# The high parts of the filling channel's weights: cast on GpSimd in place of ScalarE

## Chip, cores and metric

One core of a Trainium2 chip (trn2). The metric is the device time of one execution in microseconds (us). A program of this kernel has five instruction queues that matter here: TensorE (PE, with PEld for its weight loads), VectorE (DVE), ScalarE (ACT), GpSimd (POOL) and SyncE (SP), which issues most of the loads. Each runs its own instructions strictly in the order written into its queue, and waits where an operand is not ready.

## What is computed

A two-layer encoder over 512 tokens of width 1024. Per layer the normed input `h` is projected to five mixers (three kinds of softmax attention, a linear recurrence with a state per head, and attention over a memory of 256 tokens), each mixer's output is projected by its own rows of `w_branch` and weighted by a gate, and the sum goes through `w_out`, a residual and a layer norm:

```python
for i, (o, wdt) in enumerate(zip(branch_outs, BRANCH_WIDTHS)):
    proj = jnp.einsum('bsc,cd->bsd', o, w_branch[start:start + wdt])
    gate = jax.nn.sigmoid(jnp.einsum('bsd,de->bse', h, w_gate[:, i * d:(i + 1) * d]) + b_gate[i * d:(i + 1) * d])
    terms.append(gate * proj)
```

All of it is in float32.

## The kernel before

Every large product is done as three products of rounded operands. A weight tile arrives as float32 (`wraw`), is split into a high part (`whi`, a cast to the rounded type float32r) and a low part (`wlo`, the raw value minus the high part), and `gemm3_steps` (L145) issues for each block of 128 input rows the three matmuls high*high (L149), high*low (L150) and low*high (L151), 512 columns each.

Weights come through two channels, named by a letter: `r` for the projections that stand first in a stage, and `f` for the ones that fill: the gates and the branch projections of `branch_steps` (L370), the second projection of a pair in the first attention mixer, its `silu2`, and the memory's keys and values (`memory_kv`, L260). `load_w` (L120) loads 128x512 pieces from the SP queue into `wrawr` or `wrawf` (two buffers each); `split_w` (L129) makes the high part on ACT (L135) and the low part on DVE (L136), in `whir`/`wlor` or `whif`/`wlof`, two buffers each. A piece of 512 columns feeds four blocks, that is twelve matmuls. A buffer of `whif` is free again once its last L150 matmul is done, one of `wrawf` once its low part is made.

A layer has three parts. First the attention mixers (before 520 us, and 1110 to 1620 us in the profile). Then the recurrence (520 to 1075, and 1620 to 2170 us): `early` (L802) prepares a head pair, `late` (L945) runs a chain of small DVE operations that inverts triangular blocks (L963 multiplies into `pr`, L965 adds into `W`) and a chain of small matmuls, with many small ACT copies between. As the recurrence alone would leave PE idle, `fill` (L396) runs the gates and branch projections of four of the five mixers beside it, one block of three matmuls at a time (`pull`, L404). The gate's product stands in one PSUM buffer `pf`; ACT reads it by a Tanh (`gt`, L380), and only then the branch's product takes the same buffer. Last the fifth mixer's gates, `w_out` and the layer norm.

POOL has little: a cast of a mask table (L321), six memsets per two layers, and DMA issues (`k_stack`, L435 and L437, which copies halves of the keys across partitions, and `reload`, L366, which fetches spilled mixer outputs `o`).

The order in each queue is set by a scheduler when the program is built; it takes instructions in the order in which it believes they become ready.

Of the kernel before, what the change touches and what calls it, by code (L numbers as in the profile page):

```python
# [52 lines left out]
def encoder_kernel(ctx: ExitStack, tc: tile.TileContext, x, mem, ln_in, rel_bias, w_in, par, w_up, a_up,  # L53
                   d_lambda, w_mem, w_branch, w_gate, w_out, lnp, cst, cossin, onehot, cnt, msk, out):
    nc = tc.nc
# [30 lines left out]
    def f(t):  # L86
        return t.bitcast(F32)
# [32 lines left out]
    def load_w(src, n, ch):  # L120
        r = []
        for o in range(0, n, 512):
            w = min(512, n - o)
            raw = wp.tile([128, 512], F32, name="wraw" + ch, tag="wraw" + ch, bufs=2)[:, :w]
            nc.sync.dma_start(out=raw, in_=src[:, o:o + w])
            r.append((raw, w))
        return r

    def split_w(src, n, ch="r", raws=None):  # L129

        r = []
        for raw, w in raws or load_w(src, n, ch):
            hi = wp.tile([128, 512], F32R, name="whi" + ch, tag="whi" + ch, bufs=2)[:, :w]
            lo = wp.tile([128, 512], F32R, name="wlo" + ch, tag="wlo" + ch, bufs=2)[:, :w]
            nc.scalar.copy(hi, raw)  # L135
            tt(lo, raw, f(hi), ALU.subtract)  # L136
            r.append((hi, lo))
        return r
# [22 lines left out]
    def proj(ps, l, blk, hT, ch="r"):  # L161
        w = split_w(w_in[l, blk], 1024, ch)
        gemm3(ps, [(*wk(w, k), hT[:, 0, k, :], hT[:, 1, k, :]) for k in range(8)])

    def proj_halves(pss, l, blks, hT, chs, ws):

        ws = ws or [split_w(w_in[l, b], 1024, ch) for b, ch in zip(blks, chs)]
        for sl in (slice(0, 256), slice(256, 512)):
            for ps, w in zip(pss, ws):
                gemm3(ps[:, sl], [(*wk(w, k), hT[:, 0, k, sl], hT[:, 1, k, sl]) for k in range(8)])  # L170
# [89 lines left out]
    def memory_kv(l, b):  # L260
        ps = ps_m()
        w = split_w(w_mem[l, b], 1024, "f")
        gemm3(ps[:, :256], [(*wk(w, k), mT[k // 2][:, 0, k % 2, :], mT[k // 2][:, 1, k % 2, :]) for k in range(8)])
        kv = wp.tile([128, S], F32, name="kv", tag="gt", bufs=1)[:, :256]
        nc.scalar.copy(kv, ps[:, :256])
        nc.sync.dma_start(out=scr_kv[l, b], in_=kv)
# [1013 lines left out]
```

## Time and profile before

| | |
|---|---|
| median of 3 runs | 2260.67 us (2260.49 to 2261.9) |
| the profiled execution | 2261.37 us |
| its span, first to last instruction | 2259.6 us |
| PE / DVE / ACT / POOL busy | 97% / 77% / 56% / 3% |
| the chain that ended last | PE 70%, DVE 14%, ACT 8%, DMA 5%, issue 3% |
| the filling channel's casts on ACT | 272, 164.4 us |
| mean granted clock of PE | 0.999 of full speed (2.4 GHz) |

Around the span the profiled execution has 1.8 us. The matmuls are pipelined: two of 512 columns that follow each other start some 0.23 us apart though each shows 0.39 us, so a busy PE may still have gaps. "The chain" is followed back from the last instruction through whatever released each step; time of an engine that is not on it costs nothing by itself.

### The profile page before, as it was taken

How to read it: one execution, taken by the hardware profiler on the slowest of the kernel's cores; microseconds unless marked ns; L12 is line 12 of the kernel's file. 1: busy time of each engine (PE TensorE's matmuls, PEld its weight loads, DVE VectorE, ACT ScalarE, POOL GpSimd, SP SyncE). 2: the span in 40 equal slices, each digit the busy share in tenths (PEclk: the TensorE clock that was granted, in tenths of full speed). 3: DMA queues.
4: the chain of work that ended last, by engine and by line, in shares of the span. 5: the costliest groups of instructions: out<-in, count | busy, mean ns of one | idle time of the engine just before them, and what ended most of it. 6: DMA issues, size and time to landing. Idle time of an engine off the chain costs nothing.

```text
span 2259.6 us, 36239 instructions
## 1 busy us (share of the span) xinstructions
PE 2186.5 (97%) x13056; PEld 1678.6 (74%) x13056; DVE 1730.6 (77%) x4236; ACT 1273.2 (56%) x2785; POOL 59.6 (3%) x117
## 2 busy tenths in 40 slices
PE   6999999999999999999999999999999999999998
PEld 5777777777767777777787777777777777777776
DVE  7677887677989797975568778766788979879565
ACT  3565666676665555644326656677675646565440
POOL 0000000100000000000000000001000000000000
PEclk9999999999999999999999999999999999999999
DMA  7732124322222221315333312333313213222261
GB/s 261 222 108 91 56 80 112 113 86 85 75 80 66 86 88 59 102 49 181 117 115 108 98 62 70 97 106 89 112 57 99 71 62 98 72 80 73 84 195 38
DMA packets 111780, 220.49 MB, mean 98 GB/s; under 512 B 13240, under 2 KB 23224, under 8 KB 111216
## 3 DMA queue, kind: packets, MB, share of 16 engines
q1 hardware_dynamic: 101456, 195.09, 27.0%
q0 software_dynamic: 10144, 23.08, 4.0%
q8 instruction: 103, 1.69, 0.3%
q14 instruction: 77, 0.63, 0.1%
HBM read 187.66 MB, written 27.31 MB: 95 GB/s over the span
## 4 chain that ended last, share of the span: by engine, by line
PE 70%; DVE 14%; ACT 8%; DMA 5%; issue 3%; DVEq 0%; POOL 0%; ACTq 0%; SPq 0%
PE pg L150 10%; PE pg L151 10%; PE pg L149 10%; PE pf L149 6%; PE pf L150 5%; PE pf L151 5%; PE psc L444 4%; PE po L489 3%; PE pt L470 3%; DVE W L965 2%; DVE pr L963 2%; DMA wrawr<-in_w_out_dram 1%; DVE wlof L136 1%; PE po L479 1%; DMA wrawf<-in_w_mem_dram 1%
## 5 line engine op out<-in xcount | busy, mean ns | idle before, releaser
L149 PE MATMUL pg<-hT,whir 128*128 128x512 f32 (+1 forms) x912 | 364.0, 399 | 3.2 <-DVE kl L436 1.4
L150 PE MATMUL pg<-hT,whir 128*128 128x512 f32 (+1 forms) x912 | 365.4, 401 | 0.5 <-DVE hT L176 0.5
L151 PE MATMUL pg<-hT,wlor 128*128 128x512 f32 (+1 forms) x912 | 363.8, 399 | 2.1 <-DVE wlor L136 2.1
L136 DVE TENSOR_TENSOR wlor<-wrawr,whir 128x512 fp32r<-128x512 f32 x240 | 163.9, 688 | 114.8 <-ACT whir L135 104.9
L135 ACT CAST whir<-wrawr 128x512 fp32r<-128x512 f32 x240 | 147.7, 618 | 175.1 <-PE pg L150 116.7
L135 ACT CAST whif<-wrawf 128x512 fp32r<-128x512 f32 (+1 forms) x272 | 164.4, 605 | 135.4 <-PE pf L150 77.9
L149 PE MATMUL pf<-hT,whif 128*128 128x512 f32 x512 | 220.8, 431 | 3.4 <-DVE gt L388 2.8
L136 DVE TENSOR_TENSOR wlof<-wrawf,whif 128x512 fp32r<-128x512 f32 (+1 forms) x272 | 181.4, 669 | 49.2 <-ACT whif L135 43.2
L150 PE MATMUL pf<-hT,whif 128*128 128x512 f32 x512 | 206.7, 404 | 0.0
L151 PE MATMUL pf<-hT,wlof 128*128 128x512 f32 x512 | 205.2, 401 | 0.0
L149 PEld LDWEIGHTS pg<-hT,whir 128*128 128x128 f32 x912 | 172.0, 189 | 40.6 <-issue 3.0
L151 PEld LDWEIGHTS pg<-hT,wlor 128*128 128x128 f32 x912 | 171.9, 188 | 40.0 <-DVE wlor L136 4.9
L150 PEld LDWEIGHTS pg<-hT,whir 128*128 128x128 f32 x912 | 171.9, 189 | 37.8 <-issue 3.9
L176 DVE TENSOR_TENSOR pT<-pt,pT 128x512 fp32r<-128x512 f32 x176 | 114.2, 686 | 34.2 <-ACT pT L175 33.1
L175 ACT CAST pT<-pt 128x512 fp32r<-128x512 f32 x176 | 94.7, 589 | 63.0 <-PE pt L470 61.7
L149 PEld LDWEIGHTS pf<-hT,whif 128*128 128x128 f32 x512 | 96.5, 188 | 35.8 <-DVE gt L388 10.2
L470 PE MATMUL pt<-cst,p 128*128 128x128 f32 x704 | 118.6, 273 | 0.5 <-DVE p L461 0.5
L151 PEld LDWEIGHTS pf<-hT,wlof 128*128 128x128 f32 x512 | 96.4, 188 | 22.2 <-issue 1.6
L963 DVE TENSOR_TENSOR pr<-W,U 128x60 f32<-128x60 f32 (+24 forms) x496 | 103.5, 209 | 11.4
L965 DVE TENSOR_TENSOR W<-W,pr 128x60 f32<-128x60 f32 (+24 forms) x496 | 102.9, 208 | 11.0
L470 PEld LDWEIGHTS pt<-cst,p 128*128 128x128 f32 x704 | 89.8, 141 | 28.4 <-DVE p L461 3.6
L150 PEld LDWEIGHTS pf<-hT,whif 128*128 128x128 f32 x512 | 96.8, 189 | 18.8 <-issue 4.3
(326 smaller groups left out, 4809.1 us busy)
## 6 DMA issues: line engine op xcount, KB each, us to landing
wrawr<-in_w_in_dram SPq DMA_DIRECT2D x224, 256.0 KB, 2.8
wrawf<-in_w_gate_dram SPq DMA_DIRECT2D x160, 256.0 KB, 2.8
o<-scr_o POOLq DMA_DIRECT2D x26, 512.0 KB, 4.5
wrawf<-in_w_branch_dram SPq DMA_DIRECT2D x48, 256.0 KB, 2.7
bias<-scr_toe SPq DMA_DIRECT2D x24, 448.0 KB, 3.3
scr_o<-os SPq DMA_DIRECT2D x20, 512.0 KB, 3.7
wrawf<-in_w_in_dram SPq DMA_DIRECT2D x32, 256.0 KB, 3.0
wrawr<-in_w_out_dram SPq DMA_DIRECT2D x32, 256.0 KB, 2.9
```

Source lines behind the costliest of these rows:

```text
L135: nc.scalar.copy(hi, raw)
L136: tt(lo, raw, f(hi), ALU.subtract)
L149: mm(ps, ah, bh, start=(i == 0), stop=False)
L150: mm(ps, ah, bl, start=False, stop=False)
L151: mm(ps, al, bh, start=False, stop=(i == n - 1))
L175: nc.scalar.copy(hi, src)
L176: tt(lo, src, f(hi), ALU.subtract)
L444: mm(ps[:, :nk], q[:, i, sl], part[:, i if g is None else g, :nk], start=(j == 0), stop=(j == 1))
L470: nc.tensor.transpose(pt[:, qb * 128:(qb + 1) * 128], p4[qb][:, kb * 128:(kb + 1) * 128], ident)
L489: mm(po, vwin(kb), pT[:, b, :], start=(kb == 0 and b == 0), stop=(kb == nkb - 1 and b == 1))
L963: tt(pr, W[:, t8, s:s + 1].to_broadcast([128, nt, n]), U[:, s:s + 1, rsl].to_broadcast([128, nt, n]), ALU.mult)
L965: tt(W[:, t8, rsl], W[:, t8, rsl], pr, ALU.add)
```

## The change

```diff
-            nc.scalar.copy(hi, raw)
+            if ch == "f":
+                nc.gpsimd.tensor_copy(hi, raw)
+            else:
+                nc.scalar.copy(hi, raw)
             tt(lo, raw, f(hi), ALU.subtract)
```

The 272 casts of channel `f` go from ACT's queue to POOL's; the 240 of channel `r` stay on ACT. Lines after L134 stand three higher in the changed kernel. The scheduler orders all queues anew.

ACT's queue in the middle of the recurrence of the first layer, where the Tanh of a gate stands at 829.46 us. Before:

```order
L1088 CAST yhi<-ys 128x512
L893 COPY NS<-pm 32x2x32
L890 COPY NS<-pm 32x128
L893 COPY NS<-pm 32x2x32
L890 COPY NS<-pm 32x128
L135 CAST whif<-wrawf 128x512
L380 ACTIVATE gt<-pf,hb 128x512
L893 COPY NS<-psc 32x2x32
```

and now:

```order
L1091 CAST yhi<-ys 128x512
L896 COPY NS<-pm 32x2x32
L893 COPY NS<-pm 32x128
L896 COPY NS<-pm 32x2x32
L893 COPY NS<-pm 32x128
L383 ACTIVATE gt<-pf,hb 128x512
L896 COPY NS<-psc 32x2x32
```

The cast that stood between the copies and the Tanh is gone, and nothing else has moved there.

POOL's queue from the start of the first recurrence to the second layer's first key copy. Before:

```order
L728 MEMSET WD 128x1024
L732 MEMSET ST_5175 128x128
L732 MEMSET ST_5176 128x128
L366 DMA o<-scr_o 128x1024 x13
L435 DMA kh<-kh 64x512
```

and now (the first rows of it):

```order
L731 MEMSET WD 128x1024
L735 MEMSET ST_5175 128x128
L735 MEMSET ST_5176 128x128
L136 CAST whif<-wrawf 128x512 x15
L369 DMA o<-scr_o 128x1024 x4
L136 CAST whif<-wrawf 128x512 x24
L369 DMA o<-scr_o 128x1024 x4
L136 CAST whif<-wrawf 128x512 x24
L369 DMA o<-scr_o 128x1024 x2
```

The casts stand between the reloads. Ten fill casts stand ahead of the memsets and fifteen behind, and the first mixer has 24, so the first gate piece of each following mixer is cast ahead of that mixer's reloads and the second piece behind them.

DVE's queue inside the inversion chain, at about 796 us. Before:

```order
L136 TENSOR_TENSOR wlof<-wrawf,whif 128x512
L965 TENSOR_TENSOR W<-W,pr 128x3x23
L963 TENSOR_TENSOR pr<-W,U 128x66
L965 TENSOR_TENSOR W<-W,pr 128x3x22
L963 TENSOR_TENSOR pr<-W,U 128x63
L965 TENSOR_TENSOR W<-W,pr 128x3x21
L963 TENSOR_TENSOR pr<-W,U 128x60
L965 TENSOR_TENSOR W<-W,pr 128x3x20
L136 TENSOR_TENSOR wlof<-wrawf,whif 128x512
```

and now:

```order
L139 TENSOR_TENSOR wlof<-wrawf,whif 128x512
L1048 COPY ST_5176<-pt 64x64
L1058 TENSOR_TENSOR SY<-pt,SY 64x256 x2
L966 TENSOR_TENSOR pr<-W,U 128x66
L968 TENSOR_TENSOR W<-W,pr 128x3x22
L966 TENSOR_TENSOR pr<-W,U 128x63
L968 TENSOR_TENSOR W<-W,pr 128x3x21
L966 TENSOR_TENSOR pr<-W,U 128x60
L968 TENSOR_TENSOR W<-W,pr 128x3x20
L966 TENSOR_TENSOR pr<-W,U 128x76
L968 TENSOR_TENSOR W<-W,pr 128x4x19
L139 TENSOR_TENSOR wlof<-wrawf,whif 128x512
```

The low parts stand a few places to either side of where they were, still among the steps of the chain.

## Rows read from the trace of the kernel before

**Rows 1.** The page: busy time of each engine, the chain by engine.

```profile
PE 2186.5 (97%) x13056; PEld 1678.6 (74%) x13056; DVE 1730.6 (77%) x4236; ACT 1273.2 (56%) x2785; POOL 59.6 (3%) x117
...
PE 70%; DVE 14%; ACT 8%; DMA 5%; issue 3%; DVEq 0%; POOL 0%; ACTq 0%; SPq 0%
```

**Rows 2.** Stretches: length, busy PE, PEld, DVE, ACT, POOL; clock, DMA share, GB/s.

```profile
170.00:520.00 350.00, 346.85 (x1628) 267.98 (x1627) 268.13 (x619) 229.83 (x474) 14.27 (x28) 1.00 0.30 89
520.00:1075.00 555.00, 539.18 (x3877) 404.69 (x3876) 446.58 (x1182) 314.44 (x734) 8.29 (x16) 1.00 0.28 88
...
1620.00:2170.00 550.00, 534.13 (x3856) 400.75 (x3855) 444.25 (x1177) 312.40 (x731) 8.35 (x16) 1.00 0.28 87
```

**Rows 3.** The page's groups: count, busy us, mean ns, idle time before and its releaser.

```profile
L135 ACT CAST whif<-wrawf 128x512 fp32r<-128x512 f32 (+1 forms) x272 | 164.4, 605 | 135.4 <-PE pf L150 77.9
...
L136 DVE TENSOR_TENSOR wlof<-wrawf,whif 128x512 fp32r<-128x512 f32 (+1 forms) x272 | 181.4, 669 | 49.2 <-ACT whif L135 43.2
```

**Rows 4.** The two recurrences, ACT's instructions on tile whif alone.

```profile
520.00:1075.00 555.00, 56.77 (x95) 1.00 0.28 88
1620.00:2170.00 550.00, 56.00 (x94) 1.00 0.28 87
```

**Rows 5.** The chain by line, in 520 to 1075 us and in 1620 to 2170 us.

```profile
by line: PE pf L149 11.0%; PE pf L150 9.0%; PE pf L151 9.0%; issue 4.1%; PE pg L150 4.0%; DVE W L965 3.9%; PE pg L151 3.9%; DVE pr L963 3.8%; PE pg L149 3.8%; DMA wrawr<-in_w_out_dram 2.7%; DVE wlof L136 2.3%; PE psc L881 2.0%; DMA wrawr<-i
...
by line: PE pf L149 11.3%; PE pf L150 9.4%; PE pf L151 9.3%; issue 4.0%; PE pg L150 4.0%; DVE W L965 3.9%; PE pg L151 3.9%; DVE pr L963 3.8%; PE pg L149 3.8%; DVE wlof L136 2.3%; DMA wrawr<-in_w_out_dram 2.2%; PE psc L881 2.0%; PE pm L881 1
```

**Rows 6.** Waits: us in total, times, longest us.

```profile
PE pf L149 <- ACT gt L380: 5.0, 12, 0.7
...
DVE wlof L136 <- ACT whif L135: 43.2, 39, 3.4
...
ACT whif L135 <- PE pf L150: 77.9, 72, 4.5
```

**Rows 7.** Timeline of DVE, POOL, PE about POOL's only cast: start, length, instruction.

```profile
21.57 1.28 DVE L236 SCALAR_TENSOR_TENSOR xt<-xt,lnmv,lngb 128x1024 f32<-128x1024 f32 x1
...
21.99 1.85 POOL L321 CAST msk<-mk 128x1152 bf16<-128x1152 f32 x1 [21.55 <-DMA mk<-in_msk_dram]
...
22.77 1.11 DVE L187 TENSOR_SCALAR rsy<-lnmv 128x2 int32<-128x2 int32 x1
...
24.52 0.39 PE L151 MATMUL pg<-hT,wlor 128*128 128x256 f32 x1 [1.19 <-DVE wlor L136]
```

**Rows 8.** POOL's memsets by shape; then L187's durations (ns min/median/max).

```profile
L728 POOL MEMSET WD<- 128x1024 f32 x2 | 2.0, 991 | 112.3 <-DMA wrawr<-in_w_in_dram 56.3 <-DVE cf L719 56.0
...
L732 POOL MEMSET ST<- 128x128 f32 x4 | 0.8, 214 | 0.0
...
L187 DVE TENSOR_SCALAR rsy<-lnmv x8: 145/156/1106, 8.6 to 2253.2; 128x2 int32<-128x2 int32 x4, 128x1 int32<-128x1 int32 x4
```

**Rows 9.** DVE in 520 to 1075 us: tiles W, wlof and wlor alone.

```profile
520.00:1075.00 555.00, 117.11 (x528) 1.00 0.28 88
...
520.00:1075.00 555.00, 62.58 (x95) 1.00 0.28 88
...
520.00:1075.00 555.00, 25.19 (x37) 1.00 0.28 88
```

**Rows 10.** The chain in order of time: start, length, what.

```profile
785.80 0.23 PE pf L151
...
828.81 0.62 ACT whif L135
...
829.46 0.70 ACT gt L380
```

**Rows 11.** Timeline at a reload: second gate cast, last issue, the gate's first matmul.

```profile
788.74 0.62 ACT L135 CAST whif<-wrawf 128x512 fp32r<-128x512 f32 x1 [0.28 <-DVE W L965]
...
789.24 0.54 POOL L366 DMA_DIRECT2D o<-scr_o  x1 [0.97 <-PE pt L1042]
...
789.94 0.50 PE L149 MATMUL pf<-hT,whif 128*128 128x512 f32 x1
```

## The prediction

> **What bounds the kernel now.** I read the page first [rows 1]: PE is busy for 97% of the span and carries 70% of the chain, DVE 14%, ACT 8%. ACT is the engine that is relieved, so the question is where ACT holds anything up, and what POOL, idle for 97%, does to others when it works. By stretches [rows 2] the attention part (170 to 520 us) is PE's: 346.85 of 350 us, so that neither a lighter ACT nor a slower DVE moves much there. The recurrences are different. PE is busy there too, but DVE is at 446.58 of 555 us, and the chain by line [rows 5] goes through DVE's small steps: W 3.9%, pr 3.8%, and the low part of the filling channel 2.3%. These two stretches also hold 95 and 94 of the 272 casts [rows 4]. So the recurrences decide, and in them DVE is the engine to watch, more than ACT. The granted clock is 1.00 in all three stretches, which is the level of 2.4 GHz, and plays no part.
>
> **What the change removes.** 272 casts of 605 ns, 164.4 us of ACT's time, and ACT's idle time ahead of them, 135.4 us, of which 77.9 us in 72 waits for PE to give a buffer of whif back [rows 3, 6]. Nothing behind such a cast on ACT could run in that time. What this is worth is what of it lies on the chain. In rows 5 the casts are not among the lines shown, the smallest of which is 2.0%; so they are at most 2.0% of 555 us and of 550 us, 22 us in both. Not all of that is given back: where the next step of the chain is the low part on DVE, the cast is needed all the same, on whichever engine. It is given back where the next step is another ACT instruction, as at 828.81 us [rows 10]: the cast, then the gate's Tanh, for which PE waits; there the Tanh would have come 0.62 us earlier. PE's waits for that Tanh are small in total, 5.0 us in 12 [rows 6]. I take a gain of 10 us, a little under half the bound, and keep 0 and 22 as its ends.
>
> **What it adds on POOL.** One row shows a POOL instruction that reads SBUF, the cast of the mask table, 1152 columns in 1.85 us [rows 7]. Scaled by columns to 512 that is 0.82 us. But it began at 21.99 us while DVE's L236, which reads two SBUF operands, ran until 22.85; from there to the cast's end at 23.84 there are 0.99 us. POOL's memsets take 991 ns for 1024 columns and 214 for 128 [rows 8], 0.87 ns a column, by which 1152 columns are 1.10 us. So I read the cast as 0.86 us of waiting for DVE and 0.99 us of work: 0.86 ns a column, 0.44 us for 512, and with some 0.1 us that the memsets show beyond their columns (214 less 128 x 0.87) 0.54 us. The ends are 0.54 and 0.82; I take 0.55, as the memsets' rate fits it. Alone, then, a cast on POOL is no dearer than the 0.605 us on ACT.
>
> **What it adds on DVE.** The same rows show the price. L187, a DVE instruction on 128x2 numbers, began at 22.77, took 1.11 us, where its median is 0.156 [rows 7, 8], and ended at 23.88, 0.04 us behind POOL's cast. The next DVE instruction, a low part, came late, and PE waited 1.19 us for it [rows 7]. So a reading POOL instruction and a DVE instruction held each other up, first DVE the cast, then the cast DVE, each for its whole length. The Trainium skill says so too (SBUF — State Buffer, "Who interferes with whom"): a DVE instruction with two SBUF inputs contends with a GpSimd instruction that reads SBUF, and whichever comes first keeps the other out to its end. The trace agrees for the case above, and shows the case of a two-input instruction that is itself kept out nowhere. If only L187's kind were kept out, by the trace alone, the sum would be that of the first rival below.
>
> In 520 to 1075 us the DVE time on tiles W, wlof and wlor alone is 117.11, 62.58 and 25.19 us [rows 9], all instructions with two SBUF inputs: 205 us, 37% of the stretch, a lower bound, as other products of SBUF tiles are not in it. Of this the chain holds 3.9 + 3.8 + 2.3 = 10.0% of the stretch [rows 5], again a lower bound; I put the other end at twice that. The terms:
>
> - On the chain. 189 casts x 15% (between 10 and 20) x 0.55 us = 16 us; ends 189 x 10% x 0.54 = 10 and 189 x 20% x 0.82 = 31.
> - Off the chain. A further 37 - 15 = 22% of 189 casts, 42 x 0.55 = 23 us of DVE delay, which meets 108 us of DVE idle time per recurrence. I take a third, 8 us; ends 0 and 23.
> - The other 83 casts stand where PE is the chain or a load is; 3 us, ends 0 and 5.
> - High parts that come later. DVE waits 39 times for whif [rows 6]. Each now has to wait out a DVE instruction (half of 0.67 us in about half the cases, 0.17 us), less the 0.05 us by which the cast is shorter: 39 x 0.12 = 5 us, of which I count half, 2; ends -3 (POOL is free sooner than ACT was) and 10.
>
> **What stands behind the casts on POOL.** The reloads and the key copies. A reload needs the last product of the mixer before it, so a cast written behind it would wait too. The order shows the first gate piece ahead of the reloads and the second behind. At 789.24 us the last issue takes 0.54 us [rows 11]; the second piece's cast would start at 789.8 in place of 788.74, and the twelve matmuls of the first piece (12 x 0.23 = 2.8 us from 789.94 [rows 10, 11]) cover it. I count 0, and 1 us a boundary, 6 in all, if that cover is gone. A load on SP waits for the low part as before. The new order of the queues as a whole (fill shifted a few steps within the recurrence) I cannot cost: 0, with 5 us to either side.
>
> **Sum.** 16 + 8 + 3 + 2 - 10 = +19 us on the profiled execution's 2261.4 us, 2280; its run lies 0.7 us above the median of 2260.67, so 2279 (+0.8%).
>
> **Rivals.**
> - Faster: two-input DVE instructions are not held up. Then the 1.85 us of the mask's cast are its own, a cast takes 0.82 us, DVE's 39 waits grow by 0.2 us each (8 us, half of it felt: 4), and ACT's gain counts up to its bound: 4 - 15 = -11, some 2250 us. For it: L236 ran its usual 1.28 us beside the cast; ACT's queue does block, 77.9 us. Against: the memsets' rate, and L187.
> - No difference: the held-up steps fall into DVE's idle time, the on-chain share is at its low end of 10 us, and ACT gives 10 back: 2261 us.
> - Much slower: a cast holds 0.82 us, at each of them DVE, at 80% busy, loses the whole of it, and the recurrence, a chain of DVE steps, can't make it up: 31 + 23 + 5 + 10 + 6 - 10 = +65, 2325 us. It decides from the point where DVE's idle time of 108 us per recurrence no longer lies where the casts fall.
>
> **Chances and range.** The forecast (2266 to 2300 us) 0.48, much slower 0.17, no difference 0.15, faster 0.20. Leaving out about a tenth on each side: 2250 to 2318 us; the likeliest case alone is 2266 to 2300. A measurement can tell some 0.2% (4.5 us) from no change: faster 0.20, same 0.15, slower 0.65.
>
> **What would show it.** Right: POOL busy up by 150 us or more, its casts between 0.55 and 1.2 us long with the longer ones beside two-input DVE work; DVE's mean for W and pr above 0.21 us, or gaps ahead of them that POOL ends; DVE's share of the chain up from 14%, ACT's down from 8% by about half a point; PE's busy time unchanged but its gaps in the recurrences longer. Wrong: W and pr at their old means beside the casts (then the first rival), the two recurrences as long as before, or the time lost in the attention part, which would mean POOL's queue and not DVE.

## The result: 2.4% slower, and the profile after

The changed kernel takes 2313.95 us (median of 4 runs, 2311.86 to 2314.4) against 2260.94 us (4 runs) of the kernel before on the same chip: ratio 1.0236, 95% interval 1.0224 to 1.0249, or +53 us. The sign was right, and the outer range (2250 to 2318 us) holds the time, near its upper end. The likeliest case (2266 to 2300 us) does not hold it, and the size was wrong: +53 us where the sum gave +19.

The page after, busy time by engine and the chain by engine; these answer to [rows 1]:

```profile
PE 2204.3 (95%) x13056; PEld 1691.6 (73%) x13056; DVE 1776.5 (77%) x4236; ACT 1131.0 (49%) x2513; POOL 265.9 (12%) x389
...
PE 68%; DVE 17%; issue 6%; ACT 5%; DMA 3%; POOL 1%; SPq 0%; DVEq 0%; ACTq 0%; POOLq 0%
```

POOL took over 206 us, ACT gave up 142. On the chain ACT fell from 8 to 5% and DVE rose from 14 to 17%. PE is 95% busy in place of 97, so it waits more. The groups that answer to [rows 3] (columns: busy us, mean ns, idle time before and its releaser), with the two steps of the inversion chain:

```profile
L136 POOL CAST whif<-wrawf 128x512 fp32r<-128x512 f32 (+1 forms) x272 | 206.7, 760 | 1477.3 <-PE pf L153 949.5
...
L139 DVE TENSOR_TENSOR wlof<-wrawf,whif 128x512 fp32r<-128x512 f32 (+1 forms) x272 | 182.4, 671 | 61.2 <-POOL whif L136 51.0
...
L968 DVE TENSOR_TENSOR W<-W,pr 128x60 f32<-128x60 f32 (+24 forms) x496 | 114.4, 231 | 12.4
L966 DVE TENSOR_TENSOR pr<-W,U 128x60 f32<-128x60 f32 (+24 forms) x496 | 109.9, 222 | 12.5
```

The list of waits after (us in total, times, longest us), which answers to [rows 6]:

```profile
DVE wlof L139 <- POOL whif L136: 51.0, 53, 3.2
...
PE pf L152 <- DVE gt L391: 17.3, 18, 1.5
...
PE pf L152 <- ACT gt L383: 4.8, 13, 0.7
...
PE pg L152 <- DMA o<-scr_o: 3.9, 3, 1.9
```

DVE waits for the high part a little longer than before (51.0 us against 43.2), and PE for DVE's product gt (17.3 us; 2.8 in the trace before). PE hardly waits for ACT's Tanh, before or after. The last line is new: PE waits 3.9 us for reloaded mixer outputs, whose issues stand behind casts in POOL's queue.

How POOL and DVE hold each other up is seen in the timeline of the changed kernel in the first recurrence (start, length, instruction):

```profile
580.69 0.54 DVE L840 TENSOR_SCALAR tmp<-tmp,cf 128x512 f32<-128x512 f32 x1
...
580.93 2.21 POOL L136 CAST whif<-wrawf 128x512 fp32r<-128x512 f32 x1 [14.92 <-PE pf L153]
...
581.24 0.69 DVE L835 TENSOR_TENSOR tmp<-tmp 128x512 f32<-128x512 f32 x1
...
581.94 0.69 DVE L841 TENSOR_TENSOR tmp<-tmp,k 128x512 f32<-128x512 f32 x1
...
582.54 0.63 DVE L968 TENSOR_TENSOR W<-W,pr 128x28 f32<-128x28 f32 x1
```

The cast, 0.615 us when undisturbed, is kept out by a row of DVE instructions on SBUF tiles and ends after 2.21 us. The step on W that meets its working part takes 0.63 us where its kind takes about 0.2. I summed, over all DVE instructions, what each took beyond the median of its form in the trace before, where that was over 60 ns: 43.3 us in 126 instructions, 115 of them beside a cast of the filling channel (the kernel before has 2.4 us in 5 by the same count). The forecast of how much DVE would be delayed, read as 16 + 23 + 3 = 42 us, is therefore met in sum. Even felt in full, 43 us would not make a loss of 53.

### The profile page after: what moved, and what is told of

It reads as the page before. It is cut to its first block, busy times and chain, and to the rows that moved or that the text cites. A ratio compares the mean times of both kernels' runs of the same rounds, so it can differ in the third digit from the quotient of the medians.

```text
span 2310.1 us, 36467 instructions
## 1 busy us (share of the span) xinstructions
PE 2204.3 (95%) x13056; PEld 1691.6 (73%) x13056; DVE 1776.5 (77%) x4236; ACT 1131.0 (49%) x2513; POOL 265.9 (12%) x389
## 4 chain that ended last, share of the span: by engine, by line
PE 68%; DVE 17%; issue 6%; ACT 5%; DMA 3%; POOL 1%; SPq 0%; DVEq 0%; ACTq 0%; POOLq 0%
PE pg L154 9%; PE pg L153 9%; PE pg L152 9%; PE pf L152 6%; PE pf L153 5%; PE pf L154 5%; PE psc L447 4%; PE po L492 3%; PE pt L473 3%; DVE W L968 2%; DVE pr L966 2%; DVE wlof L139 1%; PE pt L1027 1%; PE pt L1038 1%; PE psc L152 1%
## 5 line engine op out<-in xcount | busy, mean ns | idle before, releaser
L136 POOL CAST whif<-wrawf 128x512 fp32r<-128x512 f32 (+1 forms) x272 | 206.7, 760 | 1477.3 <-PE pf L153 949.5
L152 PE MATMUL pf<-hT,whif 128*128 128x512 f32 x512 | 224.9, 439 | 24.0 <-DVE gt L391 17.3
L138 ACT CAST whir<-wrawr 128x512 fp32r<-128x512 f32 x240 | 147.9, 620 | 191.7 <-PE pg L153 120.9
L154 PEld LDWEIGHTS pg<-hT,wlor 128*128 128x128 f32 x912 | 173.1, 190 | 45.2 <-DVE wlor L139 11.1
L968 DVE TENSOR_TENSOR W<-W,pr 128x60 f32<-128x60 f32 (+24 forms) x496 | 114.4, 231 | 12.4
L966 DVE TENSOR_TENSOR pr<-W,U 128x60 f32<-128x60 f32 (+24 forms) x496 | 109.9, 222 | 12.5
```

Source lines behind the costliest of these rows:

```text
L136: nc.gpsimd.tensor_copy(hi, raw)
L152: mm(ps, ah, bh, start=(i == 0), stop=False)
L154: mm(ps, al, bh, start=False, stop=(i == n - 1))
L966: tt(pr, W[:, t8, s:s + 1].to_broadcast([128, nt, n]), U[:, s:s + 1, rsl].to_broadcast([128, nt, n]), ALU.mult)
L968: tt(W[:, t8, rsl], W[:, t8, rsl], pr, ALU.add)
```

## Experiments

Each compares with runs of the kernel before on the same chip. All of them fix the order of some or all queues. To do so a table of the wanted order is written into the kernel, and at the end of the program each instruction of a queue is tied behind the one that shall stand ahead of it, in issue order alone. Instructions named in `_EXTRA` are left out of the table; the scheduler places them. The core of it, cut from the function that reads the table:

```diff
+            if last is not None:
+                tc.add_manual_dep(ins[i], last.name,
+                                  mybir.DependencyInfo(mybir.DependencyClass.NoSync, mybir.DependencyReason.DATA),
+                                  reason="queue")
+            last = ins[i]
```

How much the change had moved: counting the fewest instructions that must be shifted to turn the old order into the new, 1553 of 10804 on PE, 847 of 4108 on DVE, 286 of 2240 on ACT, 66 of 704 on SP.

### The casts on POOL, the old order

> The casts of channel f stand on POOL, as in the changed kernel, but every instruction of PE, DVE, ACT and SP stands in its queue where it stands in the kernel before (a table of the old order is written into the kernel; POOL's own order is free). Theory A (the step of the prediction that took the new order of the queues at 0 is what failed): the casts alone cost what the prediction's other terms gave, +19 us, so 2275 to 2290, and the remaining 25 to 38 us of the 53 are gone. Theory B (the order costs nothing, POOL's and DVE's holding each other up costs all): 2305 to 2320 as in the changed kernel.

2284.2 us, ratio 1.0110 (1.0095 to 1.0125): +24.7 us. So the step itself costs about what the prediction's other terms said (+19), and the new order costs as much again, 53.0 - 24.7 = 28 us. Theory B falls. The table itself costs nothing: in the run with memsets below, which writes the old order in the same way, the time is that of the kernel before.

### The new order, the casts on ACT

> The reverse: the casts of channel f are back on ACT, and every other instruction of PE, DVE, SP, POOL and ACT stands where it stands in the changed kernel; where the casts go among ACT's instructions is free. Theory A (the order): the kernel stays slow, 2285 to 2300, though no cast is on POOL. Theory B (the hold-ups of POOL and DVE): back at 2261, within 5 us.

2353.5 us, ratio 1.0416 (1.0398 to 1.0433): slower than the changed kernel, and beyond what either theory said. The order that the scheduler made for casts on POOL does not suit casts on ACT. Its list of waits:

```profile
DVE wlof L136 <- ACT whif L135: 120.9, 75, 6.8
...
PE pf L149 <- ACT gt L380: 12.3, 26, 1.3
```

DVE waits 120.9 us for ACT's high parts in place of 43.2 [rows 6]. The time is far from the 2261 us of theory B, but the run says little on the price of the order: where the casts go on ACT was left free, and they came late. (POOL's own order was left to the scheduler here too; the table holds PE, DVE, ACT and SP.)

### POOL occupied, and nothing else changed

```diff
             nc.scalar.copy(hi, raw)
+            if ch == "f":
+                d = wp.tile([128, 512], BF16, name="dum", tag="dum", bufs=1)[:, :w]
+                _EXTRA.add(nc.gpsimd.tensor_copy(d, f(hi)).ins.name)
```

> The kernel before in its own order, with one instruction more per cast: after ACT has made a high part of channel f, POOL copies it (128x512, float32 in, bf16 out to halve the space) into a tile that nobody reads. No engine but POOL waits for these 272 copies, beyond the release of the high part's buffer some 3 us later, so what they cost is the hold-up of DVE by a busy POOL alone. If the prediction's terms for that are right (16 + 8 + 3): +27 us, 2280 to 2295. If the hold-ups fall into DVE's idle time: 2261 to 2268. If the hold-ups explain the whole loss by themselves: 2305 or more.

2287.9 us, ratio 1.0126 (1.0111 to 1.0141): +28.4 us, where the three terms for the hold-up said 27. So near an agreement is partly chance, as the copies meet other DVE work than the casts do: a copy starts when ACT has made the high part, just when DVE makes the low part of the same piece. By the count of delays above, 18.7 of 53.8 us fell on wlof here, while with the casts on POOL in the old order 24.2 of 45.7 us fell on W and pr. The copies were then made half as wide:

```diff
-                d = wp.tile([128, 512], BF16, name="dum", tag="dum", bufs=1)[:, :w]
-                _EXTRA.add(nc.gpsimd.tensor_copy(d, f(hi)).ins.name)
+                d = wp.tile([128, 256], BF16, name="dum", tag="dum", bufs=1)
+                _EXTRA.add(nc.gpsimd.tensor_copy(d, f(hi[:, 0:256])).ins.name)
```

> As d_copy (28 us for 272 copies of 512 columns), with copies of 256 columns. If what it costs goes with the time that POOL holds: 0.55 to 0.6 of it, since a copy has a fixed part: 15 to 18 us, 2274 to 2280. If a hold counts each time, whatever its length: 25 us or more. If short holds fall into DVE's idle time: under 8 us.

2271.2 us, ratio 1.0064 (1.0049 to 1.0079): +13.5 us, 0.48 of the whole copies' price and less than the 15 to 18 us expected, which had counted a fixed part of each copy as holding DVE. And the copies were replaced by a write that reads nothing, made to wait for ACT's cast as the copies do:

```diff
-            nc.scalar.copy(hi, raw)
+            cast = nc.scalar.copy(hi, raw)
+            if ch == "f":
+                d = wp.tile([128, 384], F32, name="dum", tag="dum", bufs=1)
+                x = nc.gpsimd.memset(d, 0.0).ins
+                tc.add_manual_dep(x, cast.ins.name,
+                                  mybir.DependencyInfo(mybir.DependencyClass.Sync, mybir.DependencyReason.DATA),
+                                  reason="after the cast")
+                _EXTRA.add(x.name)
```

> As d_copy, but POOL's extra instruction after each cast of ACT is a memset of 128x384 float32 into a tile that nobody reads: POOL writes SBUF and reads nothing. By the memsets of the kernel before (991 and 214 ns for 1024 and 128 columns, 0.87 ns a column and 103 ns) it takes 0.44 us, against 0.62 for an undisturbed copy. If POOL's writing holds DVE up as its copies do: 28 x 0.44 / 0.62 = 20 us, 2275 to 2285. If only POOL's reading does, or both together: 2258 to 2264.

2259.1 us, ratio 1.0006 (0.9996 to 1.0015): nothing. The durations (ns, min/median/max) of one DVE line, a 128x512 product of two SBUF operands that often falls beside these POOL instructions, in the kernel before, with whole copies, with half copies and with memsets:

```profile
L825 DVE TENSOR_TENSOR tmp<-tmp x16: 683/691/693, 554.1 to 2036.8; 128x512 f32<-128x512 f32 x16
```

```profile
L828 DVE TENSOR_TENSOR tmp<-tmp x16: 678/1103/1127, 554.7 to 2063.2; 128x512 f32<-128x512 f32 x16
```

```profile
L828 DVE TENSOR_TENSOR tmp<-tmp x16: 678/888/912, 552.6 to 2047.4; 128x512 f32<-128x512 f32 x16
```

```profile
L832 DVE TENSOR_TENSOR tmp<-tmp x16: 682/691/693, 551.8 to 2034.1; 128x512 f32<-128x512 f32 x16
```

A copy of 512 columns adds 0.41 us to the median, one of 256 columns 0.20, a memset nothing. The delay of DVE summed as above is 53.8 us with whole copies, 26.1 with half ones, 45.7 in the old order with the casts themselves. The run times rise by 28.4, 13.5 and 24.7, each time a little over half of it.

### ACT occupied

```diff
             nc.scalar.copy(hi, raw)
+            if ch == "f":
+                d = wp.tile([128, 512], BF16, name="dum", tag="dum", bufs=1)[:, :w]
+                _EXTRA.add(nc.scalar.copy(d, f(hi)).ins.name)
```

> The kernel before in its own order, with ACT copying each high part of channel f once more into a tile that nobody reads (128x512, float32 in, bf16 out), 272 copies of about 0.6 us more in ACT's queue: the mirror of what the change takes from ACT. The prediction gave that relief 10 us, with ends of 0 and 22. If an occupied ACT costs as much as that: 2264 to 2280. If ACT's time is free at the margin: within 3 us of 2258. The place of the copies in ACT's queue is the scheduler's.

2277.9 us, ratio 1.0082 (1.0068 to 1.0095): +19 us. An ACT that is occupied longer does cost. It does not follow that an ACT that is relieved gives as much back: the casts on POOL in the old order cost as much as hold-ups alone do (24.7 us for 45.7 us of DVE delay, against 28.4 for 53.8), so relief and later high parts together come to about nothing. This takes a microsecond of DVE delay to cost the same in both runs, which no run tested.

### Which queue carries the order's 28 us

> The changed kernel (casts of channel f on POOL) with PE's queue alone put back into the order of the kernel before; DVE, ACT, SP and POOL are ordered by the scheduler around it. q_before_pool, with all four queues put back, took 2284 us, the changed kernel 2314. If the loss of 29 us that the order makes is in PE's queue: 2280 to 2290. If it is in DVE's and ACT's: 2305 or more. In between if both carry it.

2316.0 us, ratio 1.0256 (1.0240 to 1.0271): +58 us, nothing is won as a whole.

> The changed kernel with DVE's and ACT's queues put back into the order of the kernel before, PE's and SP's free. If the 29 us are in DVE's and ACT's order: 2280 to 2290. If they are in PE's: 2305 or more, unless PE's order follows by itself, since what PE can run hangs on what DVE and ACT make: it then lies within some 5 us of q_before_pool.

2295.8 us, ratio 1.0176 (1.0160 to 1.0192): +38 us, about half of the 28 us is won. The time lies between the two expectations.

> The changed kernel with parts of the old order: PE's queue as in the kernel before inside the two recurrences only, DVE's and ACT's as in the kernel before outside of them only (start, attention, end); everything else is ordered by the scheduler. Stage by stage, the kernel with PE's old order lost 12 us in each recurrence but 10 and 12 us in the attention parts, the one with DVE's and ACT's old order 17 us in each recurrence but about 0 and 2 in the attention parts. If the order's loss is made in two places (PE's queue in the recurrences, DVE's and ACT's in the attention parts), the parts add up to 12 + 12 + 0 + 2 = 26 us: 2280 to 2292. If the two can't be taken apart by stage (what is shifted in one comes back in the other): 2300 or more.

2295.9 us, ratio 1.0167 (1.0151 to 1.0183): +37 us, between the two expectations, so the parts don't quite add up. No queue put back alone wins the whole loss back. A table by stretch says more. The marks are the scans of the recurrence (`nc.vector.tensor_tensor_scan` in `early`, eight a layer); lengths in us between their starts, from the traces:

| kernel | start to scan 2 | 2 to 3 | 3 to 8 | 8 to scan 2, layer 2 | 2 to 3 | 3 to 8 | to the end |
|---|---|---|---|---|---|---|---|
| before | 572.0 | 57.9 | 307.5 | 732.8 | 58.0 | 307.4 | 224.1 |
| after | 578.0 | 70.6 | 314.0 | 740.1 | 70.1 | 314.0 | 223.2 |
| casts on POOL, old order | 570.7 | 59.5 | 314.2 | 738.1 | 59.7 | 312.2 | 228.2 |
| PE in old order | 582.1 | 59.0 | 316.1 | 746.5 | 59.2 | 315.2 | 231.7 |
| DVE, ACT in old order | 570.8 | 59.6 | 316.1 | 741.3 | 60.2 | 316.0 | 230.0 |

Of the 27 us between the second row and the third, 11.1 and 10.4 lie between scan 2 and scan 3 of the two layers, 58 us of the program each, and 7.3 ahead of the second scan of the first layer; the last stretch gives 5.0 back. Both partly restored kernels have the short stretch from scan 2 to 3 back. PE's old order alone loses elsewhere what it wins there: ahead of the second scans (582.1 and 746.5 us) and in the last stretch (231.7).

What stands in that stretch is seen in the matmuls on tile pf alone, the fill (stretch, length, PE busy and count on pf). Before, up to scan 2 and from scan 2 to 3, in both layers:

```profile
0.00:572.40 572.40, 53.51 (x186) 1.00 0.39 121
572.40:630.40 58.00, 24.07 (x91) 1.00 0.20 60
1250.00:1670.40 420.40, 53.43 (x185) 1.00 0.29 89
1670.40:1728.40 58.00, 24.19 (x91) 1.00 0.20 60
```

And after:

```profile
0.00:578.40 578.40, 43.86 (x148) 0.99 0.38 119
578.40:649.20 70.80, 34.99 (x134) 1.00 0.21 64
1250.00:1703.00 453.00, 44.28 (x154) 1.00 0.29 88
1703.00:1773.20 70.20, 33.69 (x129) 1.00 0.21 65
```

Some 38 fill matmuls of the first layer, and 31 of the second, that stood ahead of scan 2 now stand behind it. At 0.23 us each [rows 10] the 43 more between scan 2 and 3 are 9.9 us, most of the 12.8 by which the stretch grew. PE's time in the same stretches, all matmuls, before:

```profile
520.00:572.40 52.40, 51.57 (x268) 1.00 0.28 92
572.40:630.40 58.00, 55.26 (x414) 1.00 0.20 60
```

and after:

```profile
525.00:578.40 53.40, 49.25 (x245) 0.94 0.25 80
578.40:649.20 70.80, 69.58 (x482) 1.00 0.21 64
```

Ahead of scan 2 PE now stands idle for 4.2 us in place of 0.8, at a mean granted clock of 0.94. Behind it PE is the bound, 98% busy, with fill that it could have done earlier.

The same part of each layer in all kernels, from the first fill matmul to the third scan (us, from the traces):

| kernel | layer 1 | layer 2 |
|---|---|---|
| before | 410.9 | 411.0 |
| after | 426.2 | 426.9 |
| casts on POOL, old order | 412.7 | 412.0 |
| PE in old order | 414.7 | 414.5 |
| DVE, ACT in old order | 411.9 | 412.7 |
| parts of the old order | 413.9 | 412.8 |

Against the old order the changed kernel loses 13.5 and 14.9 us here, as much as the order costs in all. With PE's queue alone put back the fill stands where it stood:

```profile
0.00:582.40 582.40, 53.39 (x185) 0.99 0.37 119
582.40:641.20 58.80, 24.19 (x91) 1.00 0.20 63
```

and 11.5 and 12.4 us of it are won. With DVE's and ACT's queues put back PE's order follows by itself there: 186 and 91 fill matmuls. The run with PE's old order won nothing as a whole because it loses 24 us elsewhere against the changed kernel, where PE's old order stands beside a new one of the other queues: 4.0 ahead of the first fill matmul, 10.0 between the third scan and the next layer's fill, 9.7 behind the third scan of the second layer.

To test this, the old order of PE, DVE and ACT was put back in that part of each layer alone:

> The changed kernel with the old order of PE, DVE and ACT in one stretch of each layer alone: from the first fill matmul (219 us in the trace of before, 1317 in the second layer) to the third scan of the recurrence (635 and 1733). The rest is free. By the two profiles the changed kernel lost 15.5 us from 170 to 630 us and 16 in the same stretch of the second layer, q_before_pool 1.8 and 1.0; by the second scan 148 fill matmuls were done in place of 185, and 131 in place of 91 stood between the second and the third. If the shifted fill makes the order's loss: 53 - 14 - 15 = 24 us over before, 2278 to 2290. If the rest of the order matters as much, or the loss comes back behind the stretch: 2298 or more.

2287.2 us, ratio 1.0122 (1.0106 to 1.0137): +27.7 us, 25 of the 28 us are back, with everything ahead of the first fill matmul and behind the third scan left to the scheduler. The fill stands where it stood:

```profile
0.00:571.50 571.50, 53.15 (x185) 1.00 0.39 121
571.50:630.00 58.50, 24.36 (x92) 1.00 0.21 64
```

From the first fill matmul to the third scan it takes 412.1 and 413.3 us. So the order's loss is made in these two parts, and most of it in PE's queue, since PE's old order alone wins 24 of the 28 us there. That the shifted fill is what makes it is likely but not shown: other matmuls changed their places with it, and no run moved the fill alone. A part goes by the clock. In these two parts the granted clock was 0.50 for 10.2 us in the changed kernel and never in the old order, which is at most 5 of the 28 us (an estimate: half of 10.2).

### A cast on POOL only where DVE is not pressed

```diff
-            if ch == "f":
+            if ch == "f" and not fills:
                 nc.gpsimd.tensor_copy(hi, raw)
```

The rest of the edit, cut here, sets `fills` at the two calls of `branch_steps`.

> As q_before_pool (the old order of PE, DVE, ACT and SP), but only the 48 casts of the attention's second projections and of the memory's keys and values stand on POOL; the 224 of the gates and the branches go back to ACT. The stretch up to the first recurrence ended 1.6 us earlier in q_before_pool than before, and the second attention part took as long as before. If POOL's casts gain where ACT is the busier engine: 2253 to 2257, faster than both kernels. If the 1.6 us were the scatter of one profile: 2257 to 2260, no difference.

2259.3 us, ratio 1.0002 (0.9993 to 1.0011): no difference. The 1.6 us are not found again.

### A faster kernel: memsets to POOL

```diff
-                        nc.vector.memset(WD[tg[u], :, sg[u]], 0.0)
+                        nc.gpsimd.memset(WD[tg[u], :, sg[u]], 0.0)
```

> A try at a kernel faster than both: the kernel before in its own order, casts on ACT, with the 32 memsets of WD in late (L976, 8.7 us on DVE, 0.27 us each) on POOL, since d_memset showed that POOL's writing does not hold DVE up. DVE's chain in the recurrences is shorter by them: 8.7 us x about 0.6 (the share of DVE's delay that the run time showed in d_copy) = 5 us, 2251 to 2256. If the memsets lie beside other work anyway: 2257 to 2260. Slower, 2265 or more, if a memset waits behind a reload in POOL's queue.

2254.8 us, ratio 0.9976 (0.9966 to 0.9985): 4.6 us faster than the kernel before, and so faster than both. The line in its trace:

```profile
L976 POOL MEMSET WD<- x32: 302/304/311, 522.9 to 2075.9; 32x256 f32 x32
```

A memset takes 304 ns on POOL, longer than the 272 that it took on DVE in the kernel before, and never more than 311: no DVE instruction kept it out. What POOL is given here writes only.

## Why the prediction was off, step by step

**The step that failed** is the last one of the part on POOL's queue: "The new order of the queues as a whole (fill shifted a few steps within the recurrence) I cannot cost: 0, with 5 us to either side." The runs showed 28 us in its place, more than the whole of the rest: 53.0 us with the new order, 24.7 with the casts on POOL in the old one. Both halves of the sentence were wrong. The fill is not shifted a few steps within the recurrence: 38 matmuls of it in the first layer and 31 in the second go out of the stretch ahead of the second scan into the next. And the bound of 5 us had no row behind it. The orders of the two programs could be read before any run: in PE's queue 179 fill matmuls stand ahead of the ninth matmul of L881 in the recurrence before, and 144 after. At 0.23 us each the 38 and 31 matmuls are 8.7 and 7.1 us of PE work, put into a stretch in which PE is 98% busy: 16 of the 28 us, if each costs its time. What makes the other 12 is open, but for at most 5 by the clock. I looked at a few places where little had moved, a cast gone from ACT's queue and low parts a few places off, and took them for the whole.

**On the chain, off the chain, other casts (16 + 8 + 3 = 27).** Confirmed in sum, by luck in part. Copies that do nothing but hold DVE up cost 28.4 us, though they hit other DVE work than the casts. The pieces were less good: the hold is 0.41 to 0.44 us, not 0.55, and more DVE instructions were hit, among them TENSOR_SCALARs, which the prediction's 37%, a lower bound, left out. (That share has an error of its own: 13.9 of the 117.11 us on W are 32 transposes with one operand.) The cast's record is 0.613 to 0.617 us long, so some 0.2 us of it holds nobody. The working in the prediction had 0.44 us (0.86 ns a column) and then added the 0.1 us that memsets show beyond their columns to the hold, where it does not belong.

**High parts that come later (+2) and ACT's relief (-10).** Together about 0 in place of -8. They can't be told apart from these runs. DVE's waits for the high part are the same in the old order (42.6 us against 43.2), so the relief was probably the smaller one, but that is argued, not shown.

**The reloads (0, up to 6 if the cover is gone).** PE waits 3.9 us in 3 waits for reloaded tiles, 2.6 us in the old order; none stood among the waits of before. So the term is not 0 but within its ends; what these waits cost in time was not measured.

**The rivals.** Two-input instructions on DVE are held up, so "faster" falls for the reason that spoke against it. "Much slower" gave 2325 us, near the result, and is still not what happened. Its mechanism, a hold of 0.82 us felt in full, is excluded by the half that is felt and by 0.44 us. "No difference" needed the hold-ups to fall into DVE's idle time; copies alone cost 28.4 us.

**What would show it.** POOL's busy time rose by 206 us, the casts' longer ones lie beside DVE products, W rose to a mean of 231 ns and pr to 222, and DVE's share of the chain rose from 14 to 17%, as foretold. But these signs hold in the old order as well, at half the loss. Other signs missed: 12 casts took longer than 1.2 us, up to 3.9; ACT's share of the chain fell by 3 points and not by half a point; PE's busy time rose by 18 us. The sign that was missing from the list is a count of the fill done by a given point of the recurrence.

## What to carry to other kernels

When a scheduler orders the queues, a change of engine is two changes, and the second can be the larger: compare the two orders by counting how much of each filling kind of work stands ahead of fixed marks, multiply the difference by its price, and give the order a term of its own with a wide range: here the count gave 16 of 28 us. To take the two changes apart, fix the old order and change the engine alone. A GpSimd instruction that reads SBUF was paid for by DVE instructions on SBUF operands, 0.41 us for a 128x512 copy beside a product of two, while memsets beside such products were free: send memsets to GpSimd, not casts, where DVE is near the chain, and look first at what DVE does beside them.

## What the runs showed of the hardware

- The hold follows the columns that POOL reads, not the length of its record: 0.20 us for 256 columns, 0.41 for 512, while the undisturbed records (128x256 and 128x512) are about 0.40 and 0.61 us long. DVE products with one operand in PSUM (SY from pt, 64x256; gt from pf, 128x512) that started beside a copy took their usual time, within 10 ns. The Trainium skill (SBUF — State Buffer, "Who interferes with whom") says that a DVE instruction with two SBUF inputs contends with a GpSimd instruction that reads SBUF and not with one that only writes. The trace agrees: the memsets added nothing to a median of 691 ns.
- Products of two SBUF operands are not all that is held up. The scaling of p, a TENSOR_SCALAR of 128x512, never took over 490 ns before and up to 839 beside a cast:

```profile
L461 DVE TENSOR_SCALAR p<-p,sst x160: 333/481/490, 57.5 to 1610.2; 128x512 f32<-128x512 f32 x144, 128x256 f32<-128x256 f32 x16
```

```profile
L464 DVE TENSOR_SCALAR p<-p,sst x160: 334/481/839, 61.5 to 1639.0; 128x512 f32<-128x512 f32 x144, 128x256 f32<-128x256 f32 x16
```

- Nor is every memset free. In the kernel before, small TENSOR_SCALARs that came up beside POOL's memset of WD, 0.17 us long in the first layer, lasted in the second until the memset's end:

```profile
1621.37 0.99 POOL L728 MEMSET WD<- 128x1024 f32 x1 [56.03 <-DVE cf L719]
1621.38 1.01 DVE L720 TENSOR_SCALAR cf<-cf 128x14 f32<-128x14 f32 x1
```

- POOL did not get in between DVE instructions on SBUF tiles that follow each other closely. Of the 272 casts 75 took over 0.7 us, and the longest:

```profile
L136 POOL CAST whif<-wrawf x272: 400/615/3917, 14.3 to 2245.1; 128x512 fp32r<-128x512 f32 x128, 128x256 fp32r<-128x256 f32 x8
```

- A wait of PE can cost twice. In the changed kernel two scalings of xt and an instruction held up by POOL's mask cast stand ahead of a low part in DVE's queue, and PE waits 3.20 us for it. PE alone in two stretches, the wait and what followed (busy and count, granted clock), after:

```profile
21.50:24.60 3.10, 0.00 (x0) 1.00 0.03 8
25.60:31.90 6.30, 6.30 (x24) 0.50 0.46 171
```

and before:

```profile
21.50:24.60 3.10, 1.91 (x15) 1.00 0.29 89
25.60:31.90 6.30, 6.30 (x49) 1.00 0.40 155
```

Behind the idle stretch the granted clock was 0.50, the level of 1.2 GHz, and PE ran 24 matmuls (6144 columns) where it ran 49 (10368 columns) at 2.4 GHz before. The prediction said that the clock plays no part; over the whole span the mean granted clock fell from 0.999 to 0.994, with five stretches at 0.50 that the kernel before does not have, 23.9 us in all.
